# Split GELU-multiply on one core: GELU in place, the wait for the output tile on VectorE, closing clears merged

## Chip, cores, metric

One core of a Trainium2 chip. The metric is device time in microseconds of one execution. Beside it each run gives the core's *span*, from its first to its last profiled instruction; the time is a little longer than the span. In profile lines DVE is VectorE, ACT ScalarE and SP SyncE (with a q: that engine's sequencer, which runs waits and issues transfers); a semaphore is a counter by which one engine or transfer tells another that it is done.

## The reference

```python
# x: (32, 512, 2048) float32 -> out: (32, 512, 1024) float32
x1, x2 = x[..., :1024], x[..., 1024:]
out = 0.5 * x1 * (1 + erf(x1 / sqrt(2))) * x2
```

134.2 MB are read and 67.1 MB written, once each.

## The kernel before

The 16,384 rows are cut into 16 tiles of 128 partitions x 8 rows. Input tile `x` (64 KB per partition) and output tile `o` (32 KB) exist twice, so tiles i and i+2 share a buffer: there are two interleaved chains, one per parity. SyncE issues the loads, ScalarE runs the GELU and issues most stores, VectorE does the product.

```python
for i in range(n_tiles):
    k = i % 2
    last = i == n_tiles - 1
    pieces = i == 0 or last
    steps = ((0, 2), (2, 4), (4, 8)) if pieces else ((0, 5), (5, 8))
    if i >= 2:
        nc.scalar.wait_ge(stored[k], n[stored[k].name])    # o buffer free?
    for lo, hi in steps:
        rows = slice(lo, hi)
        ...                                                # first/loaded: x there?
        counted(nc.scalar.activation(out=o_bufs[k][:, rows, :],
                in_=x_bufs[k][:, rows, :half], func=GELU), gelu_done, 1)
        nc.vector.wait_ge(gelu_done, n[gelu_done.name])
        counted(nc.vector.tensor_mul(out=o_bufs[k][:, rows, :],
                in0=o_bufs[k][:, rows, :], in1=x_bufs[k][:, rows, half:]), mul_done, 1)
        ...                                # first and last tile: store each half
    ...                                    # else: store tile i once product is done
    if i + 2 < n_tiles:
        nc.sync.wait_ge(mul_done, n[mul_done.name])
        load(i + 2, slice(0, R), loaded[k])
nc.scalar.drain()
for sem in (first, *loaded, *stored):
    nc.scalar.sem_clear(sem)
nc.vector.drain()
nc.vector.sem_clear(gelu_done)
...                                        # SyncE waits for the last stores
```

Of the kernel before, what the change touches and what calls it, by code (L numbers as in the profile page):

```python
# [1 line left out]

# [4 lines left out]

GELU = mybir.ActivationFunctionType.Gelu


@with_exitstack
def kernel(
    ctx: ExitStack,
    tc: tile.TileContext,
    x: bass.AP,
    out: bass.AP,
):
    nc = tc.nc
    P = nc.NUM_PARTITIONS

    x_flat = x.flatten_outer_dims()
    out_flat = out.flatten_outer_dims()
    n_rows, dim = x_flat.shape
    half = dim // 2

    R = 8
    x_t = x_flat.rearrange("(n p r) d -> n p r d", p=P, r=R)
    o_t = out_flat.rearrange("(n p r) d -> n p r d", p=P, r=R)
    n_tiles = x_t.shape[0]
    x_bufs = [nc.alloc_sbuf_tensor(f"x{k}_tile", [P, R, dim], x.dtype) for k in range(2)]  # L30
    o_bufs = [nc.alloc_sbuf_tensor(f"o{k}_tile", [P, R, half], out.dtype) for k in range(2)]

    first = nc.alloc_semaphore("first")
    loaded = [nc.alloc_semaphore(f"loaded{k}") for k in range(2)]
    stored = [nc.alloc_semaphore(f"stored{k}") for k in range(2)]
    gelu_done = nc.alloc_semaphore("gelu_done")
    mul_done = nc.alloc_semaphore("mul_done")
    tail_stored = nc.alloc_semaphore("tail_stored")
    n = {sem.name: 0 for sem in [first, *loaded, *stored, gelu_done, mul_done, tail_stored]}

    def counted(ins, sem, by):
        ins.then_inc(sem, by)
        n[sem.name] += by

    def load(i, rows, sem):
        counted(
            nc.sync.dma_start(out=x_bufs[i % 2][:, rows, :], in_=x_t[i][:, rows, :]), sem, 16  # L47
        )

    def store(queue, i, rows, sem):  # L50
        queue.wait_ge(mul_done, n[mul_done.name])
        counted(
            queue.dma_start(out=o_t[i][:, rows, :], in_=o_bufs[i % 2][:, rows, :]), sem, 16
        )



    with tc.tile_critical():  # L58
        load(0, slice(0, 4), first)
        load(0, slice(4, 8), loaded[0])  # L60
        load(1, slice(0, 8), loaded[1])
    tc.close()
    tc.compile()  # L63

    for i in range(n_tiles):
        k = i % 2
        last = i == n_tiles - 1
        pieces = i == 0 or last
        steps = ((0, 2), (2, 4), (4, 8)) if pieces else ((0, 5), (5, 8))
        if i >= 2:  # L70
            nc.scalar.wait_ge(stored[k], n[stored[k].name])
        for lo, hi in steps:
            rows = slice(lo, hi)
            if i == 0 and lo == 0:
                nc.scalar.wait_ge(first, n[first.name])
            elif lo == 0 or (i == 0 and lo == 4):
                nc.scalar.wait_ge(loaded[k], n[loaded[k].name])
            counted(
                nc.scalar.activation(  # L79
                    out=o_bufs[k][:, rows, :], in_=x_bufs[k][:, rows, :half], func=GELU  # L80
                ),
                gelu_done,
                1,
            )
            nc.vector.wait_ge(gelu_done, n[gelu_done.name])
            counted(
                nc.vector.tensor_mul(  # L87
                    out=o_bufs[k][:, rows, :],
                    in0=o_bufs[k][:, rows, :],
                    in1=x_bufs[k][:, rows, half:],  # L90
                ),
                mul_done,
                1,
            )
            if pieces and hi % 4 == 0:
                if last:
                    store(nc.sync, i, slice(hi - 4, hi), tail_stored)
                else:
                    store(nc.scalar, i, slice(hi - 4, hi), stored[k])
        if not pieces:  # L100
            if i == n_tiles - 2:
                store(nc.sync, i, slice(0, R), tail_stored)
            else:
                store(nc.scalar, i, slice(0, R), stored[k])
# [3 lines that stand above are left out]


    nc.scalar.drain()  # L110
    for sem in (first, *loaded, *stored):
        nc.scalar.sem_clear(sem)
    nc.vector.drain()
    nc.vector.sem_clear(gelu_done)
    nc.sync.sem_clear(mul_done)
    nc.sync.wait_ge(tail_stored, n[tail_stored.name]).then_inc(
        tail_stored, -n[tail_stored.name]
    )


# [1 line left out]
_INS = ['x']  # L122
_OUTS = [((32, 512, 1024), 'float32')]


# [23 lines left out]
```

## Time and profile before

| | before |
|---|---|
| median time (first three runs: 469.56, 469.59, 471.63) | 469.59 us |
| span of the profiled run | 468.1 us |
| VectorE, ScalarE busy | 140.5, 115.5 us |
| moved | 201.3 MB, 430 GB/s over the span |

The DMA issues, with the size of each transfer and the median time from its issue to its landing:

```profile
out_dram<-o_tile ACTq DMA_DIRECT2D x13, 4096.0 KB, 44.7
...
x_tile<-in_x_dram SPq DMA_DIRECT2D x15, 44.5
```

A 4 MB store takes as long to land as the 8 MB load beside it (44.7 and 44.5 us), and far longer than its bytes need: 4.19 MB at the 434 GB/s of the middle stretches are 9.7 us. So most of the 44.7 us is a place in a queue (an estimate from these figures).

### The profile page before, as it was taken

How to read it: one execution, taken by the hardware profiler on the slowest of the kernel's cores; microseconds unless marked ns; L12 is line 12 of the kernel's file. 1: busy time of each engine (PE TensorE's matmuls, PEld its weight loads, DVE VectorE, ACT ScalarE, POOL GpSimd, SP SyncE). 2: the span in 40 equal slices, each digit the busy share in tenths (PEclk: the TensorE clock that was granted, in tenths of full speed). 3: DMA queues.
4: the chain of work that ended last, by engine and by line, in shares of the span. 5: the costliest groups of instructions: out<-in, count | busy, mean ns of one | idle time of the engine just before them, and what ended most of it. 6: DMA issues, size and time to landing. Idle time of an engine off the chain costs nothing.

```text
span 468.1 us, 174 instructions
## 1 busy us (share of the span) xinstructions
DVE 140.5 (30%) x34; ACT 115.5 (25%) x35; POOL 0.2 (0%) x4
## 2 busy tenths in 40 slices
DVE  0330514207052060511606116060150702507043
ACT  1320606032060410604106050050500506014060
POOL 0000000000000000000000000000000000000000
DMA  8999899999999999999999999999999999999998
GB/s 358 448 448 442 375 423 496 414 403 445 417 482 403 420 431 493 403 403 448 470 426 403 442 409 493 403 403 448 493 403 403 448 442 454 404 428 423 493 395 367
DMA packets 5041, 201.34 MB, mean 430 GB/s; under 512 B 560, under 2 KB 560, under 8 KB 560
## 3 DMA queue, kind: packets, MB, share of 16 engines
q1 hardware_dynamic: 2880, 142.61, 70.5%
q10 hardware_dynamic: 2160, 58.72, 29.1%
q14 instruction: 1, 0.01, 0.0%
HBM read 134.22 MB, written 67.11 MB: 430 GB/s over the span
## 4 chain that ended last, share of the span: by engine, by line
DMA 76%; DVE 14%; ACT 8%; ACTq 0%; SPq 0%; issue 0%
DMA out_dram<-o_tile 66%; DVE o_tile L87 14%; DMA x_tile<-in_x_dram 10%; ACT o_tile L79 8%; ACTq L110 0%; SPq L47 0%; SPq L63 0%; SPq L58 0%
## 5 line engine op out<-in xcount | busy, mean ns | idle before, releaser
L87 DVE TENSOR_TENSOR o_tile<-o_tile,x_tile 128x5120 f32<-128x5120 f32 (+3 forms) x34 | 140.5, 4170 | 320.2 <-ACT o_tile L79 320.2
L79 ACT ACTIVATE o_tile<-x_tile 128x5120 f32<-128x5120 f32 (+3 forms) x34 | 114.3, 3407 | 337.4 <-DMA out_dram<-o_tile 301.9
L79 ACT ACT_TABLE_LOAD x1 | 1.3, 1283 | 3.3 <-PEq L63 3.3
L133 POOL MEMSET const-bfloat16-1.0<- 128x1 bf16 x1 | 0.1, 102 | 0.0
L133 POOL MEMSET const-uint8-127<- 128x1 uint8 x1 | 0.1, 102 | 0.0
L133 POOL MEMSET const-float32-1.0<- 128x1 f32 x1 | 0.1, 99 | 0.0
L133 POOL MEMSET const-float32-0.0<- 128x1 f32 x1 | 0.1, 98 | 0.2 <-issue 0.2
## 6 DMA issues: line engine op xcount, KB each, us to landing
out_dram<-o_tile ACTq DMA_DIRECT2D x13, 4096.0 KB, 44.7
x_tile<-in_x_dram SPq DMA_DIRECT2D x2, 4096.0 KB, 16.7
out_dram<-o_tile ACTq DMA_DIRECT2D x2, 2048.0 KB, 34.4
out_dram<-o_tile SPq DMA_DIRECT2D x1, 4096.0 KB, 25.1
out_dram<-o_tile SPq DMA_DIRECT2D x2, 2048.0 KB, 7.6
x_tile<-in_x_dram SPq DMA_DIRECT2D x15, 44.5
```

The lines of the kernel that those rows point to most:

```text
L79: nc.scalar.activation(out=o_bufs[k][:, rows, :], in_=x_bufs[k][:, rows, :half], func=GELU),
L87: nc.vector.tensor_mul(out=o_bufs[k][:, rows, :], in0=o_bufs[k][:, rows, :], in1=x_bufs[k][:, rows, half:],),
L133: nc = _bacc.Bacc("TRN2", target_bir_lowering=False, num_devices=1)
```

## The change

The intent: let ScalarE start a tile as soon as its input is there, because writing the GELU over the input's first half needs no free output tile; let VectorE, the first to write the output tile, wait for that; and shorten the closing instructions. The clears change with the wait: VectorE now clears the semaphores that it waits on.

```diff
-        if i >= 2:
-            nc.scalar.wait_ge(stored[k], n[stored[k].name])
         for lo, hi in steps:
...
                 nc.scalar.activation(
-                    out=o_bufs[k][:, rows, :], in_=x_bufs[k][:, rows, :half], func=GELU
+                    out=x_bufs[k][:, rows, :half], in_=x_bufs[k][:, rows, :half], func=GELU
                 ),
...
+            if i >= 2 and lo == 0:
+                nc.vector.wait_ge(stored[k], n[stored[k].name])
             nc.vector.wait_ge(gelu_done, n[gelu_done.name])
             counted(
                 nc.vector.tensor_mul(
                     out=o_bufs[k][:, rows, :],
-                    in0=o_bufs[k][:, rows, :],
+                    in0=x_bufs[k][:, rows, :half],
                     in1=x_bufs[k][:, rows, half:],
...
     nc.scalar.drain()
-    for sem in (first, *loaded, *stored):
-        nc.scalar.sem_clear(sem)
+    nc.scalar.sem_clear(range(first.num, loaded[1].num + 1))
     nc.vector.drain()
-    nc.vector.sem_clear(gelu_done)
+    nc.vector.sem_clear(range(stored[0].num, gelu_done.num + 1))
```

## The prediction

> **What bounds the kernel now.** I read the front page first: its line of slices and its DMA queues say which resource is never idle.
>
> ```profile
> DVE  0330514207052060511606116060150702507043
> ACT  1320606032060410604106050050500506014060
> ...
> DMA  8999899999999999999999999999999999999998
> ...
> q1 hardware_dynamic: 2880, 142.61, 70.5%
> q10 hardware_dynamic: 2160, 58.72, 29.1%
> ...
> HBM read 134.22 MB, written 67.11 MB: 430 GB/s over the span
> ```
>
> VectorE and ScalarE are busy 30% and 25% of 468.1 us; the 16 DMA engines are at nine tenths or more in all but three slices, and the two queues' packets fill 70.5 + 29.1 = 99.6% of them. Then the stretches view, cut at the period of one tile, shows whether anything is lost inside:
>
> ```profile
> 76.00:105.00 29.00, 8.76 (x2) 7.12 (x3) 0.00 (x0) 1.00 1.00 434
> 105.00:134.00 29.00, 8.76 (x2) 7.12 (x3) 0.00 (x0) 1.00 1.00 434
> 134.00:163.00 29.00, 8.76 (x2) 7.13 (x3) 0.00 (x0) 1.00 1.00 434
> ```
>
> Columns: window, length, busy VectorE, ScalarE, GpSimd, clock, DMA share, GB/s. A tile moves 8.39 MB in and 4.19 MB out, 12.58 MB; 12.58 / 0.434 = 29.0 us. The period is the transfer time.
>
> The chain of waits, in order of time, must then be read with care:
>
> ```profile
> 60.60 40.06 DMA out_dram<-o_tile
> 100.66 0.02 issue
> 100.68 4.48 ACT o_tile L79
> 105.16 0.02 issue
> 105.18 8.77 DVE o_tile L87 x2
> 113.95 0.02 issue
> 113.98 44.67 DMA out_dram<-o_tile
> 158.65 0.02 issue
> 158.67 4.48 ACT o_tile L79
> ```
>
> It looks like a latency loop: store, GELU, two products, store, 57.99 us for two tiles. But 44.67 us is no service time: 4.19 MB at 434 GB/s need 9.7 us, and store i together with load i+2, issued at the same moment (113.97 and 113.98), need 29.0. The rest is queueing behind the other parity's pair. That pair was issued at 84.97 and lands at 129.66. So when this parity issues again at 113.98, 129.66 - 113.98 = **15.7 us** of transfers are still queued. The compute part of a tile, 13.3 us (100.66 to 113.98), could grow by 15.7 us before the DMA engines ran dry, and its shrinking gives nothing.
>
> [...] a load of 8.39 MB on one queue and a store of 4.19 MB on the other, issued together, land 0.17 to 0.18 us apart (load's last semaphore update at 100.48, store's at 100.66). [...]
>
> **The change part by part.** The operations' own rows, by form:
>
> ```profile
> L87 DVE TENSOR_TENSOR o_tile<-o_tile,x_tile 128x5120 f32<-128x5120 f32 x14 | 76.9, 5491 | 279.8 <-ACT o_tile L79 279.8
> L79 ACT ACTIVATE o_tile<-x_tile 128x5120 f32<-128x5120 f32 x14 | 62.6, 4469 | 301.1 <-DMA out_dram<-o_tile 280.1 <-DMA x_tile<-in_x_dram 21.0
> ```
>
> Columns: instruction and shapes, count, busy us, mean ns, idle before and what ended it.
>
> *GELU in place.* No instruction is added or removed: 34 ACTIVATEs and 34 products as before, same element counts, same transfers. ScalarE's output becomes runs of 1024 floats, as its input always was; VectorE's first operand becomes such runs, as its second was. [...] 0 ns each.
>
> *The wait moves.* ScalarE waited for load and store; 14 times the store was last, by 0.17 to 0.18 us. Now the GELU starts when the load lands, so 0.18 us sooner. VectorE checks the store instead, but its product cannot start until the 4.48 us GELU is over; the store has by then been in for 4.48 - 0.18 = 4.3 us. The new wait costs nothing; one wait instruction (17 ns on ScalarE) changes engine and stands ahead of a wait that is longer. The compute part falls from 13.32 to some 13.14 us. Store and next load are issued 0.18 us earlier, into a queue with 15.7 us of work; they land no earlier, and their issue-to-landing time grows from 44.67 to about 44.85. On the end: 14 x 0.18 = 2.5 us off the side, **0 us** on the path.
>
> *The last tile.* Here the queue runs out, so I looked at it alone. Load 15 lands at 448.76 and store 13 at 448.95. The last three stores are issued at 433.28, 455.43 and 460.67 and land at 458.43, 463.28 and 468.11: the last two 4.85 and 4.83 us apart, which is 2.097 MB at 432 to 434 GB/s. They too leave at the DMA rate. Packets end near 467.05, so the last store's begin near 467.05 - 4.83 = 462.2. At the kernel's start a load issued at 0.94 has packets near 1.95, 1.0 us later; so the last store must be issued by about 461.2 (an estimate from these), and is by 460.67. There are 0.5 us to spare already; 0.18 us more adds to the slack. Gain 0, at the very most 0.2.
>
> *Clears.* ScalarE's five take 46 + 4 x 41 ns, 456.25 to 456.56; four of them at 0.065 us intervals go, 0.26 us. VectorE's one at 460.73 covers three semaphores instead of one. The program ends when SyncE sees the last store at 468.12, 7.4 us later. On the path: 0.
>
> Sum: 0 + 0 + (0 to 0.2) + 0. I choose 0.1: **469.5 us**.
>
> **The rivals.** *It was ScalarE's wait that set the pace, and it gets faster.* For: the chain names the store before each GELU, and ScalarE idled 301.9 us of the span for it. Against: the load lands only 0.18 us before, so the whole wait gives 14 x 0.18 = 2.5 us on one engine, 1.26 us per parity chain of seven, even if it all counted: 468.3. And a DMA floor stands under that: 201.33 MB at 434 GB/s are 463.9 us, above the 460.2 that faster by 2% needs.
>
> *VectorE slows because both operands now lie in one tile, 4 KB apart.* For: a new pair of addresses no row here has timed. Against: [...] both are the same memory. If each product took twice its time, a tile's compute grew by 8.8 us, under the 15.7 of slack: nothing in the middle. The last tile would pay: 2.3 + 2.3 + 4.4 us, less what overlaps and 0.5 slack, some 5 to 8 us; 475 to 478, still within 2%.
>
> *The transfers slow because ScalarE now writes into the tile that loads fill.* For: 67 MB of writes change address. Against: engines already read that tile beside transfers, and 434 GB/s is held in stretches with 16 us of compute and in the tail's almost idle ones alike. I give it next to nothing.
>
> **Range and chances.** The three times before are 469.56, 469.59 and 471.63: two agree to 0.03, one is 0.4% high. The change itself is good for -0.3 to +0.1; below 469.0 I would need a gain that the DMA rate doesn't leave, above 470.6 a median that catches the odd high run. So 469.0 to 470.6. Faster by 2% lies under the DMA floor: 0.01. Slower by 2% is 9.4 us and needs more than doubled products: 0.01. Same: 0.98.
>
> **What would show it.** Right: the stretches still read 1.00 and 434; ScalarE's idle time is now ended by loads, in about the same total, some 2.5 us less; products still 5491 and GELUs 4469 ns; store issue-to-landing 44.8 to 44.9; the last store issued near 460.5 and landed near 468.1. Wrong: a product row with another mean, a product waiting for a store, a DMA share under 0.99 in a middle stretch, or last stores less or more than 4.8 us apart. What would make the number wrong is a transfer order that changes the rate, or a time from the slow side of the scatter.

## The result and the profile after

The changed kernel took 470.16 us in the median of six runs (469.87 to 472.23), against 469.60 (469.56 to 471.63) of the kernel before in as many. The ratio is 1.0012, with a 95% interval of 0.9988 to 1.0035: the same. (Ratios here are the mean time of one kernel's fast runs over the mean of the other's of the same rounds, so not quite the ratio of the medians.)

The slices and totals of the page after:

```profile
DMA  8999899999999999999999999999999999999998
...
q1 hardware_dynamic: 2880, 142.61, 70.5%
q10 hardware_dynamic: 2160, 58.72, 29.0%
```

A stretch of one tile (columns as in the prediction):

```profile
105.00:134.00 29.00, 8.76 (x2) 7.04 (x3) 0.00 (x0) 1.00 1.00 434
```

The transfers are what they were: 434 GB/s in the middle, at a DMA share of 1.00. The chain of waits, the turn that answers to the one shown of before:

```profile
100.65 0.02 issue
100.67 4.48 ACT x_tile L77
105.15 0.03 issue
105.18 0.02 DVEq L85
105.20 0.04 issue
105.25 8.77 DVE o_tile L87 x2
114.02 0.02 issue
114.03 44.74 DMA x_tile<-in_x_dram
```

The GELU is now released by the load, not the store. And there is something new between GELU and product: "DVEq L85", VectorE's sequencer running a wait instruction *after* the GELU, so that the product starts 105.25 - 105.15 = 0.10 us after the GELU's end, where before it started 0.02 us after. The groups by form:

```profile
L87 DVE TENSOR_TENSOR o_tile<-x_tile 128x5120 f32<-128x5120 f32 x14 | 76.9, 5493 | 279.9 <-ACT x_tile L77 279.9
L77 ACT ACTIVATE x_tile<-x_tile 128x5120 f32<-128x5120 f32 x14 | 62.6, 4469 | 301.0 <-DMA x_tile<-in_x_dram 301.0
```

Both operations cost what they cost before (5491 and 4469 ns), and ScalarE's idle time before these, 301.0 us against 301.1, has only changed its name. In the DMA issues, the store's time to landing has grown:

```profile
out_dram<-o_tile ACTq DMA_DIRECT2D x13, 4096.0 KB, 44.9
```

The span of the profiled run is 468.5 us. Over the six runs the spans are 468.0, 468.1, 468.1, 468.4, 468.5 and 470.4, where eleven later runs of the kernel before have 468.0 to 468.4 with one of 470.5. So most of the 0.56 us between the medians does not lie in the span. Time less span is 1.83 to 1.99 us in each of the six runs (mean 1.90), and 1.27 to 1.37 in every run of the kernel before that was taken beside the experiments (mean 1.32 to 1.34). **Some 0.57 us lie outside the span**, and the semaphore records show that they come after its end (see "The 0.57 us after the span"). The DMA records of the two traces hold one candidate. Of the instruction queue (q14), apart from what comes before the span's start (six packets of 8192 bytes in each trace), each has one 8192-byte packet:

```
kernel    instruction packet at (us)   span (us)
before    407.88                       468.1
after     470.18                       468.5
```

### The profile page after: what moved, and what is told of

Same layout as the page of the kernel before. It is cut to its first block, busy times and chain, and to the rows that moved or that the text cites. A ratio compares the mean times of both kernels' runs of the same rounds, so it can differ in the third digit from the quotient of the medians.

```text
span 468.5 us, 170 instructions
## 1 busy us (share of the span) xinstructions
DVE 140.5 (30%) x34; ACT 115.5 (25%) x35; POOL 0.2 (0%) x4
## 4 chain that ended last, share of the span: by engine, by line
DMA 75%; DVE 14%; ACT 8%; ACTq 0%; issue 0%; SPq 0%; DVEq 0%
DMA x_tile<-in_x_dram 75%; DVE o_tile L87 14%; ACT x_tile L77 8%; ACTq L110 0%; SPq L47 0%; DVEq L85 0%; SPq L63 0%; SPq L58 0%
## 5 line engine op out<-in xcount | busy, mean ns | idle before, releaser
L87 DVE TENSOR_TENSOR o_tile<-x_tile 128x5120 f32<-128x5120 f32 (+3 forms) x34 | 140.5, 4171 | 320.3 <-ACT x_tile L77 320.3
L77 ACT ACTIVATE x_tile<-x_tile 128x5120 f32<-128x5120 f32 (+3 forms) x34 | 114.3, 3407 | 337.5 <-DMA x_tile<-in_x_dram 337.5
## 6 DMA issues: line engine op xcount, KB each, us to landing
out_dram<-o_tile ACTq DMA_DIRECT2D x13, 4096.0 KB, 44.9
x_tile<-in_x_dram SPq DMA_DIRECT2D x15, 44.7
```

Source lines behind the costliest of these rows:

```text
L77: nc.scalar.activation(out=x_bufs[k][:, rows, :half], in_=x_bufs[k][:, rows, :half], func=GELU),
L87: nc.vector.tensor_mul(out=o_bufs[k][:, rows, :], in0=x_bufs[k][:, rows, :half], in1=x_bufs[k][:, rows, half:],),
```

## The experiments

Theory: the 16 DMA engines set the time, 15.7 us of queued transfers hide the compute part of each tile, and nothing in this change touches the transfers. Chief rival: the chain of waits is a latency loop, and what is added to or taken from it moves the end. Side question: where do the extra 0.57 us come from? Eleven runs (ten new kernels and the changed one again) were made; each was compared with runs of the kernel before on the same chip.

### The parts alone

**e1, clears only:** the kernel before with the diff's last part alone.

```diff
-    for sem in (first, *loaded, *stored):
-        nc.scalar.sem_clear(sem)
+    nc.scalar.sem_clear(range(first.num, loaded[1].num + 1))
     nc.vector.drain()
-    nc.vector.sem_clear(gelu_done)
+    nc.vector.sem_clear(range(stored[0].num, gelu_done.num + 1))
```

> Kernel before with only the closing clears merged. My theory (the clears end some 11 us before the last store lands): 469.6, ratio 1.000, and five clears of 41 to 46 ns on ScalarE become one. Rival for the 0.5 us by which the changed kernel came out longer (470.16 against 469.60): the merged clears cause it, then 470.1.

Measured: 469.61 us (469.43 to 469.67, five runs) against 469.50 (nine runs), ratio 1.0001 (0.9989 to 1.0014). Time less span stays at 1.33, and the instruction packet stays at 407.9. The clears are worth nothing, and by themselves they don't cause the extra time after the span.

**e2, in place only:** ScalarE keeps its wait for the store.

```diff
-   out=o_bufs[k][:, rows, :], in_=x_bufs[k][:, rows, :half], func=GELU
+   out=x_bufs[k][:, rows, :half], in_=x_bufs[k][:, rows, :half], func=GELU
-   in0=o_bufs[k][:, rows, :],
+   in0=x_bufs[k][:, rows, :half],
```

> Kernel before with only GELU written in place; ScalarE still waits for load and store, clears as before. My theory: products 5491 to 5493 ns, GELUs 4469 ns, 434 GB/s in the middle stretches, 469.6. Rival: ScalarE's writes into the tile that loads fill slow the transfers a little; then some 470.1 and DMA busy time up by 0.2 us or more.

Measured: 469.57 us (469.43 to 469.61), ratio 1.0001 (0.9988 to 1.0013). Its groups by form, and a stretch:

```profile
L87 DVE TENSOR_TENSOR o_tile<-x_tile 128x5120 f32<-128x5120 f32 x14 | 76.9, 5493 | 280.0 <-ACT x_tile L79 280.0
L79 ACT ACTIVATE x_tile<-x_tile 128x5120 f32<-128x5120 f32 x14 | 62.6, 4469 | 301.3 <-DMA out_dram<-o_tile 280.2 <-DMA x_tile<-in_x_dram 21.0
```

```profile
105.00:134.00 29.00, 8.76 (x2) 7.12 (x3) 0.00 (x0) 1.00 1.00 434
```

Two operands in one tile, a strided output, ScalarE writing where loads land: none of it shows in a duration (5493 and 4469 ns, where before has 5491 and 4469), in the rate (434 GB/s), or in the time.

**e3, in place and the wait moved,** the changed kernel with single clears:

```diff
-    nc.scalar.sem_clear(range(first.num, loaded[1].num + 1))
+    for sem in (first, *loaded):
+        nc.scalar.sem_clear(sem)
     nc.vector.drain()
-    nc.vector.sem_clear(range(stored[0].num, gelu_done.num + 1))
+    for sem in (*stored, gelu_done):
+        nc.vector.sem_clear(sem)
```

> GELU in place and the store's wait on VectorE, but the clears one by one (the two that VectorE now waits on are cleared by VectorE). My theory: time 469.6 to 470.2, the same as the changed kernel; compute part of a tile 13.38 us against 13.32. Rival: the wait's move costs the 0.5 us; then this run has it (470.1) and the in-place run does not (469.6).

Measured: 469.69 us (469.65 to 469.85), ratio 1.0005 (0.9992 to 1.0017). The spans are those of the kernel before (468.0 to 468.3), but time less span is 1.56, and the instruction packet is at 469.5. So the time fits the theory and also, at 0.2 us more than the kernel before, a part of the rival: something comes with the wait's move, but less than the changed kernel has. The compute part is 13.38 us, as expected.

**e4, the two waits swapped.** In the changed kernel the program asks for the store first and the GELU second; the profile shows the GELU's wait as the separate instruction and the store's on the product itself. This run writes them the other way round:

```diff
-            if i >= 2 and lo == 0:
-                nc.vector.wait_ge(stored[k], n[stored[k].name])
             nc.vector.wait_ge(gelu_done, n[gelu_done.name])
+            if i >= 2 and lo == 0:
+                nc.vector.wait_ge(stored[k], n[stored[k].name])
```

> Changed kernel with VectorE's two waits written in the other order, so that the store's wait should become the separate instruction and run while the GELU still runs. Theory: the 0.07 us between the end of the GELU and the product goes back to 0.02, compute part of a tile 13.38 falls to 13.32 us; the time does not move (469.6 to 470.2), because the compute part has 15.7 us to spare. Rival (the 0.07 us per tile is what made the changed kernel 0.5 us longer: 7 x 0.07 = 0.5): 0.5 us less than the changed kernel, 469.6.

Measured: 470.23 us (469.90 to 470.55), ratio 1.0016 (1.0002 to 1.0029). The chain of waits of this run:

```profile
100.51 4.48 ACT x_tile L77
104.98 0.02 issue
105.01 8.77 DVE o_tile L87 x2
113.78 0.02 issue
113.80 44.70 DMA x_tile<-in_x_dram
```

The swap works: VectorE's wait for the store now runs at 100.69, during the GELU, and the product follows 0.03 us after the GELU's end. The compute part (landing to issue) falls from 114.03 - 100.65 = 13.38 to 113.80 - 100.48 = 13.32 us. The time does not fall with it. The 0.07 us are real and cost nothing; the rival of this run is out.

### How much the queue hides

**e5 and e6** are the changed kernel with each product of the 14 middle tiles done twice and three times (result unchanged; a semaphore `again` orders the repeats, and VectorE clears it with the others):

```diff
+            for _ in range(1 if not pieces else 0):      # e6: 2
+                counted(nc.vector.tensor_mul(... the same ...), again, 1)
+                nc.vector.wait_ge(again, n[again.name])
             counted(nc.vector.tensor_mul(...), mul_done, 1)
```

> Changed kernel with each product of the 14 middle tiles done twice (same result), 8.8 to 9.0 us more in each tile's compute part: 13.4 becomes 22.3 us. Theory (15.7 us of queued transfers to spare): 469.6 to 471, DMA share still 1.00 in the middle. Rival (the chain of waits is a latency loop, seven turns per parity): 7 x 8.9 = 62 us more, 532.

Measured, e5: 471.12 us in the median of three runs (471.02, 471.12, 472.91), ratio 1.0052 (1.0034 to 1.0071). A fourth run took 478.55, over 1.5% above the fastest; it is left out.

```profile
105.00:134.00 29.00, 17.61 (x4) 7.12 (x3) 0.00 (x0) 1.00 1.00 434
```

VectorE does 17.61 us of work in a 29.00 us stretch instead of 8.76, and the DMA share is still 1.00. Over 8.8 us more per tile, 124 us of VectorE work in all, cost 1.6 us in the median where a latency loop would have cost 62. The median is 0.1 us above the range I gave. Two of the four runs are longer than the other two (spans 471.5 and 477.1 us against 469.6 and 469.7); whether that has to do with the queue, of which 6.8 us are left instead of 15.7, was not looked into and stays open.

> Changed kernel with each product of the 14 middle tiles done three times, 17.7 to 18 us more per tile: compute part 31.2 us, 2.2 us over the 29.0 at which the queue runs dry. Theory: the DMA engines stand idle some 2.2 us[...]; two tiles take 62 instead of 58 us, and filling the pipeline once more costs 15 to 25 us; 505 to 525 in all, DMA share 0.93 to 0.95 in the middle. Rivals: latency loop, 7 x 17.8 = 125 us more, 595; compute never matters, 470.

Measured, e6: 519.71 us (516.95 to 523.74), ratio 1.1066 (1.1010 to 1.1122): slower. Stretches of that run:

```profile
105.00:134.00 29.00, 21.33 (x5) 7.12 (x2) 0.00 (x0) 1.00 0.96 394
163.00:192.00 29.00, 23.88 (x6) 7.12 (x2) 0.00 (x0) 1.00 0.92 380
```

For the first time the DMA share in the middle is under 1.00 (0.89 to 0.97 in eight stretches, where I had expected 0.93 to 0.95; that figure, and the 15 to 25 us for filling the pipeline, were estimates, and no run shows the filling by itself). The first 8.8 us per tile cost 1.6 us, the next 8.8 us cost 48.6. The edge lies between, as the queue of 15.7 us says (8.9 is below it, 17.8 above). The two rivals, 595 and 470, are both out.

e6 does not show by itself that the queue ran dry first. The compute part of a tile, 31.2 us (78.90 to 110.11 in its trace), is now also longer than the 29.0 us period, and ScalarE starts a tile's GELU only after it has issued the store of the tile before (store issued at 78.49, next GELU at 78.90). ScalarE and VectorE alone would then need some 14 x 2.2 = 31 us more (an estimate from these numbers), which is over half of the 50 us. Since 29.0 = 13.3 + 15.7, both readings put the edge in the same place; no run here parts them.

**e7, an eighth of the GELU** (wrong result: 128 of each 1024 columns), which takes time away:

```diff
-   out=x_bufs[k][:, rows, :half], in_=x_bufs[k][:, rows, :half], func=GELU
+   out=x_bufs[k][:, rows, : half // 8], in_=x_bufs[k][:, rows, : half // 8], func=GELU
```

> Changed kernel with the GELU on 128 of each 1024 columns only (wrong result on purpose): the first GELU of a tile falls from 4.47 to about 0.72 us, the compute part from 13.4 to 9.6 us. Theory: 469.6 to 470.2, the store's issue-to-landing grows from 44.9 to about 48.6. The last store is issued some 3 us earlier, and lands when it did before. Rival (latency loop): 7 x 3.75 = 26 us less, 444.

Measured: 470.46 us (470.32 to 470.79), ratio 1.0021 (1.0007 to 1.0035). By form and in the DMA issues (the stretch from 105 to 134 us still has a DMA share of 1.00 and 434 GB/s):

```profile
L77 ACT ACTIVATE x_tile<-x_tile 128x640 f32<-128x640 f32 x14 | 10.3, 736 | 381.5 <-DMA x_tile<-in_x_dram 381.5
```

```profile
x_tile<-in_x_dram SPq DMA_DIRECT2D x15, 48.3
```

The tile's first GELU falls from 4.47 to 0.74 us (the 0.72 expected agrees with a line through 1901 ns at 2048 elements and 4469 at 5120, both of the kernel before, an estimate from these), and the load's time to landing rises from 44.7 to 48.3: all but 0.1 us of what was taken from the compute part turned into queueing. Nothing came off the end (spans 468.4 to 468.9). (My expectation named the store's figure. It fell to 44.6, because in this run the stores no longer land beside the loads; the loads release the GELU here, and theirs grew as expected.)

### The end

**e8, the very last product twice,** all else as in the changed kernel (the edit of e5 under another condition):

```diff
+            for _ in range(1 if last and hi == R else 0):
```

> Changed kernel with the very last product (128x4096, 4.43 us) done twice, all else as it is; the last store is issued 4.5 us later. Theory (0.5 us to spare at the end): 4.0 us more than the changed kernel, 473.5 to 474.5, and the last two stores land 8.8 us apart instead of 4.85. Rivals: the end has as much to spare as the middle, 0; or nothing to spare, 4.5.

Measured: 472.64 us (472.52 to 472.87), ratio 1.0067 (1.0053 to 1.0081). The stretches of its end:

```profile
461.00:464.00 3.00, 3.00 (x1) 0.00 (x0) 0.00 (x0) 1.00 0.41 175
464.00:467.00 3.00, 0.78 (x1) 0.00 (x0) 0.00 (x0) 1.00 0.61 257
```

Here the DMA engines do run dry, while VectorE repeats the product. The spans, 471.1 to 471.4, are 3.0 us above the usual 468.2, for 4.46 us of added work: **1.4 to 1.5 us were to spare, not 0.5.** The trace agrees by another way: with no queue ahead of it the last store (issued 464.81) is seen landed at 471.08, 6.27 us later; in the changed kernel it took 468.51 - 460.82 = 7.69. The difference, 1.42, is the queueing at the end. The last two stores land 7.9 us apart (463.14 and 471.06), not the 8.8 expected. Neither rival (0 or 4.5 us more) fits.

### The 0.57 us after the span

The wait's move makes VectorE's instruction stream longer by 14 instructions (45 to 59 in the built program) and ScalarE's shorter by 14, the clears by 4 more (79 to 61). Two runs lengthen one engine's stream alone by needless waits.

**e9:** the kernel before, with a wait on VectorE's own earlier products (always met):

```diff
+            if i >= 2 and lo == 0:
+                nc.vector.wait_ge(mul_done, n[mul_done.name])
             nc.vector.wait_ge(gelu_done, n[gelu_done.name])
```

> Kernel before with one needless wait more on VectorE in each of the 14 middle tiles (on VectorE's own earlier products, always met), so VectorE's instruction stream is as long as in the changed kernel (59 instead of 45). The 0.5 us of the changed kernel lie after the span: time less span is 1.3 us before, 1.9 changed, where an 8192-byte instruction fetch falls at 470.2 instead of 407.9. Theory V (VectorE's longer stream needs that late fetch): 470.1, time less span 1.9, a fetch near 470. Theory A (ScalarE's shorter stream moves its own fetch from 407.9 to the end): 469.5, 1.3, fetch near 408. Theory T (in the timed work itself): span up by 0.5.

**e10:** the changed kernel, with a wait on ScalarE for products that are done by then:

```diff
+        if i >= 2:
+            nc.scalar.wait_ge(mul_done, n[mul_done.name])
         for lo, hi in steps:
```

> Changed kernel with one needless wait more on ScalarE in each of the 14 middle tiles (on products it has already waited for), so ScalarE's stream is as long as in the clears-only kernel (75 instead of 61). Theory A: fetch back near 408, time less span 1.3, 469.6. Theory V: fetch near 470, time less span 1.9, 470.1.

**e11:** the changed kernel again, beside them.

> The changed kernel itself, on the same chip as the two runs above: 470.1, span 468.2, time less span 1.9, fetch near 470.2; if the 0.5 us belonged to the chip of its first runs, 469.6.

| run | VectorE, ScalarE instructions | time (median) | span (lowest to highest) | time less span (mean) | instruction packet at |
|---|---|---|---|---|---|
| before (11 runs beside these) | 45, 79 | 469.55 | 468.0 to 468.4, one 470.5 | 1.34 | 407.9 (first profile) |
| e1 clears only | 45, 75 | 469.61 | 468.1 to 468.3 | 1.33 | 407.9 |
| e9 | 59, 79 | 469.93 | 468.0 to 468.3 | 1.73 | 411.6 |
| e10 | 59, 75 | 469.91 | 468.1 to 468.3 | 1.71 | 408.0 |
| e3 | 61, 63 | 469.69 | 468.0 to 468.3 | 1.56 | 469.5 |
| e11 changed again | 59, 61 | 470.23 | 467.9 to 468.6, one 470.3 | 1.90 | 471.9 (in the run of span 470.3) |

The ratios of e9, e10 and e11 (1.0003, 1.0003 and 1.0008, all the same as the kernel before) don't part these kernels; time less span does, as it stays within 1.27 to 1.37 in every run of the kernel before. The extra time is there again in e11, in runs of its own, so it belongs to the kernel. It is no cost per instruction: e3 has two more on each engine than the changed kernel and less time after the span, 1.56.

The semaphore updates that the traces record (one trace of each run) go on after the last instruction, and they show where the time is. The last of them comes 1.45 us after the span's end in the kernel before and 1.95 in the changed one, and in eleven of the thirteen traces time less span is 0.11 to 0.13 us less than this. Two steps between the updates of semaphore 2, which none of these kernels uses itself, differ:

| step | short | long |
|---|---|---|
| between the 10th and 11th update after the end | 97 to 101 ns: before, e1, e2, e3, e5, e6, e8 (VectorE 45, 60, 61, 87, 115 instructions) | 509 to 530 ns: changed, e4, e7, e9, e10, e11 (all 59) |
| between the 6th and 7th | 34 to 35 ns: before, e1, e2, e9, e10 (ScalarE 75, 79) | 86 to 129 ns: all others (ScalarE 61, 63) |

So 0.41 us come in just the kernels whose VectorE stream has 59 instructions, and some 0.09 us in those with the shorter ScalarE stream. Together they are 0.50 of the 0.57 us. Added to the 1.33 of the kernel before, the first alone fits 1.73 and 1.71 in e9 and e10, the second alone 1.42 and 1.44 in e5 and e8. e3 is a case of its own: its long step is missing, but another group of updates starts 0.46 us later than elsewhere, and the last update comes at 1.58. The instruction packet is not what carries the 0.41 us, since e9 and e10 have the long step with the packet at 411.6 and 408.0, and e8 has no such packet at all. Why a stream of 59 is slow there and the others are not stays open.

## Why the prediction was right, and where it was not

- **The DMA engines are the bound, with 15.7 us of queue: right.** e7 takes 3.7 us out of each tile and gains nothing, e5 hides 8.9 us, e6 with 17.8 us breaks through (there the engines' own chain is over the period too, so 15.7 is worked out, and shown only to lie between 8.9 and 17.8).
- **GELU in place costs 0: right.** 5493 and 4469 ns where 5491 and 4469 were forecast; e2 alone 1.0001. That it would cost 0 was an estimate; what shows it is e2, at 3072 elements too (3352 and 2747 ns, where before has 3350 and 2747).
- **The new wait "costs nothing": right for the time, wrong in its working.** I took the added wait instruction to stand ahead of the longer wait. The build made the wait written *last* into the separate instruction and left the first on the product, so 21 ns of wait and some 0.07 us of issue around it lie between GELU and product. The profile of before could have told: there too ScalarE's separate wait (17 ns) is the one for the load, written second. From the store's landing (100.85 in the trace) to the next issue the compute part is 114.03 - 100.85 = 13.18, where 13.14 was forecast.
- **ScalarE's idle time some 2.5 us less: wrong.** It is 337.5 against 337.4 us in total. The period is set by the transfers (29.0 us a tile, at a DMA share of 1.00), and idle time is period less busy time; starting sooner only moves it.
- **Store's issue-to-landing 44.85: right,** 44.9.
- **The last tile gains nothing: right,** the last two landings are still 4.85 us apart in the changed kernel's trace. The 0.5 us to spare was the mis-sized term: 1.4 by e8. I had added the 1.0 us from issue to packets, as seen at the kernel's start, to the 1.1 us from last packet to landing; e8 shows 6.27 us in all, so 6.27 - 4.83 = 1.44 for both together. The second of them is misread: by the DMA records of the kernel before the last packet ends at 467.73, not 467.05, 0.37 us before the landing (0.35 in e8, where the first packet comes 0.82 us after the issue). The forecast issue at 460.5 was 460.82, because load 15 landed at 449.1 instead of 448.8; the landing forecast near 468.1 was 468.5.
- **Clears 0: right.** e1.
- **The number: 469.5 forecast, 470.16 measured, inside 469.0 to 470.6.** What it lacks is not in any step: 0.57 us after the span, which I took to be fixed. That the time is still in the range is luck as to this term: the upper end was set for odd high runs. A change without effect on the work still moved the time by 0.12%, in steps after the end (0.41 and some 0.09 us) that, in these thirteen traces, go with the number of instructions on VectorE and ScalarE.

## What to carry to other kernels

When the DMA share is 1.00 in every middle stretch, as here, look how much of a store's or load's time to landing is a place in a queue (here most of it: 44.7 us for bytes that need 9.7), and work out the queue's depth before calling its wait a cost: here it hid 8.9 us more per tile (15.7 by the working), and the store's wait could be moved, and most of the GELU taken out, without effect. Check by adding work, not only by removing it: two kernels with the product repeated showed between which amounts the edge lies. And if two waits precede one instruction, look which of them the build keeps on the instruction. Here it was the one written first; with the one that comes true last there, the product started 0.03 us after the GELU's end instead of 0.10 (e4), and the time stayed the same.

## What stays open

- The traces show instruction packets of 8192 bytes, one alone during or after the kernel in all profiles but e8's. The time after the span (1.32 to 1.90 us here) goes with the number of instructions on two engines in these traces; no run shows that fetching is what costs it.
- The rare longer run. Before and changed kernel alike had some runs of 471.6 to 472.2 us among those of 469.4 to 470.5. The profile of e11 caught one (span 470.3): from the second tile on, the sixteenth semaphore update of each load comes 2.2 to 2.4 us after the first, against 0.3 to 1.3 in the other profiles with the DMA engines full, and a 64 KB load packet takes 2.42 us. The lag is about the time of one packet (an estimate from these two numbers); what causes it is not shown.
